# Ordering VectorE's work in a seven-product feed-forward layer by clocks of when its operands should be there

## The chip, the cores and the metric

The kernel runs on one core of one Trainium2 chip. The metric is the device time of one execution in microseconds (us); three executions of the kernel before took 946.0, 948.33 and 948.74 us, so the median is 948.33 us. One further execution was profiled, and the durations below are from it.

## The reference, cut to what matters

The model is a trunk of two layers over 256 tokens of width 1024, in float32. Each layer is a feed-forward network, a mixer (mLSTM in the first layer, windowed attention in the second) and a second feed-forward network, each with a residual and a layer norm. The change is in the feed-forward networks, of which there are four:

```python
def swiglu(x, w_in, w_out):                      # x: 256 x 1024, w_in: 1024 x 5632, w_out: 2816 x 1024
    gu = x @ w_in
    g, u = gu[..., :D_FF], gu[..., D_FF:]        # D_FF = 2816
    return (jax.nn.silu(g) * u) @ w_out

x = layer_norm(ALPHA * x + 0.5 * swiglu(x, ffn_w_in[l, i], ffn_w_out[l, i]), ...)
```

## The kernel before, in words

**Every float32 product is three matmuls.** An operand is split into a high part (rounded to the matmul's type, a cast on ScalarE, ACT) and a low part (operand minus high part, a subtraction on VectorE, DVE). `mm3` (L517) adds high x high, high x low and low x high. Weights come from memory in pieces of 128 x 1024 elements (512 KB), and each must be loaded, cast by `high` (L220, tiles `w_hi`) and subtracted by `low` (L244, tiles `w_lo`) before TensorE (PE) can use it. There are ten buffers of `w_hi` and of `w_lo` (`RING`, L27), so the splits can run up to ten pieces ahead of PE.

**A feed-forward network** (`ffn`, L657) has an opening with ordinary products, then `down` (L800), which multiplies one chunk of 128 gated columns by its rows of w_out (12 matmuls a call, results in the `py` banks), and then four blocks of `seven` (L829). A block computes 512 gate columns and 512 up columns for both halves of the tokens with seven products instead of eight, in the manner of Strassen and Winograd: sums of parts of x (tiles `S`, made once) are multiplied by sums of parts of the weights (tiles `s_raw`, formed in place). A product (`product`, L815) is 12 matmuls of 512 columns from two pieces. After each product a small function (`end1` to `end7`, L838 to L863) copies, adds, subtracts or multiplies 128 x 512 tiles, called `e` and `g` in the profile. When the gated halves `u0` and `u1` are complete, `tr` (L677) transposes them on PE (four matmuls with `ident`), and `split_evac` (L536) writes their high part (`h_hi`, ACT) and low part (`h_lo`, DVE). These are the chunks that later calls of `down` multiply.

PE's order in a full block (the first three of a network) is: product 1, transposes of the block before's `u1`, product 2, `down`, products 5 and 6, `down`, products 7 and 3, `down`, transposes of `u0` (L877), product 4, `down`. The last block has two calls of `down` fewer and does the transposes of `u0` in `end4` (L858), behind product 4. After it the filler (below) is switched off, six rows of w_out are split at once, as many pieces of the next stage are split as have buffers, and `tail` (L612) does the last chunks and the layer norm, with the transposes of the last `u1` in its midst.

**The sums of weights.** In a block, six loaded pieces (`b11`, `b12`, `b22`, two each; tiles `s_raw`) are changed step by step, and each state of them that a product needs is split. `b11` is split, has `b12` added (DVE), is split, has `b22` added (DVE), is split, has a part of the weights added straight from memory by an accumulating DMA issued from GpSimd (POOL, L273), and is split a last time, for product 4. `b12` has such a DMA too. The list `after` (filled in the planner's `seven`, L375) tells which sum follows which split.

**The order of the splits.** All is unrolled, and each engine runs its instructions in the order in which the program emits them. `Paced` (L54) keeps a model clock for PE, DVE, ACT and the loads while the program is written, and for every tile the time at which it should be there (`when`, `mark`). While a feed-forward network is emitted, `fill` (L278) is called after every matmul and adds work for ACT and DVE, as long as their clocks are less than 300 ns (`AHEAD`) past PE's: the next `high` in the order of the plan, if its raw piece was there 1000 ns ago (`SOON`) by the clocks; the first waiting sum, on the same condition; the first waiting `low`, on the same condition. The sums, the accumulating DMAs among them, wait in one list and leave it in order. The operations of `end1` to `end7` and the `h_lo` are emitted at their place at once. `take` (L298) forces what PE needs next.

The plan's order (that of the splits) is not quite that of use. `turn` and `late` in the planner's `seven` put the last split of `b11` of one block (used by its product 4) behind the first split of `b11` of the next block (used by that block's product 1), and the program keeps a list of the order of use beside it.

Of the kernel before, what the change touches and what calls it, by code (L numbers as in the profile page):

```python
# [21 lines left out]
F = 2816  # L22
# [23 lines left out]
SOON = -1000.0  # L46
LANDING = 2200.0
LOADING = 1340.0
SECOND = 1250.0
ADDING = 8000.0  # L50
# [98 lines left out]
class Weights:  # L149
# [5 lines left out]
    def __init__(self, nc, pool, words, plan, after, turns):  # L155
        self.nc, self.pool, self.words, self.plan, self.after = nc, pool, words, plan, after
        self.raw, self.parts, self.half, self.sums = {}, {}, [], []
        self.made = self.used = self.gone = 0
        self.room = 0
        self.order, self.left = turns, set(range(len(plan)))  # L160
        self.todo = {tag: [i for i, w in enumerate(words) if w["tag"] == tag] for tag in TAGS}
        self.free = {"v_raw": 0, **{tag: 0 for tag in TAGS}, "w_raw": RAW_BUFS}
        self.spool, self.send, self.vbufs = None, 0, 0
        self.uses = [0] * len(words)
# [49 lines left out]
    def split(self, upto):  # L214
        while self.made < min(upto, len(self.plan)):
            self.high()
        while self.half and self.half[0][0] < upto:
            self.low()

    def high(self):  # L220

        nc, i = self.nc, self.made
# [18 lines left out]
        self.made += 1  # L241
        return True

    def low(self):  # L244
# [15 lines left out]
        self.sums += [(i, *sum_) for sum_ in self.after.get(i, ())]  # L260
# [3 lines left out]
    def sum(self):  # L264
        nc = self.nc
        _, w, v = self.sums.pop(0)
        t = self.raw[w]
        if isinstance(v, int):
            nc.vector.tensor_add(t, t, self.raw[v])
            self.drop(v)  # L270
            self.load()
        else:
            nc.gpsimd.dma_start(t.rearrange("p (k f) -> p k f", k=self.words[w]["k"]), v, accum_op=OP.add)  # L273
            now = max(nc.vec, nc.pe)
            nc.dma = max(nc.dma, now + LANDING) + SHARE
            nc.mark(t, now + ADDING)

    def fill(self):  # L278

        nc = self.nc  # L280
        while True:
            act, vec = max(nc.act, nc.pe), max(nc.vec, nc.pe)
            if act < nc.pe + AHEAD and len(self.half) < 2 and self.made < min(self.room, len(self.plan)):
                p = self.plan[self.made]
                if (p["word"] in self.raw and nc.when(self.raw[p["word"]]) < act + SOON
                        and not any(p["needs"] == x for x in [h[0] for h in self.half] + [s_[0] for s_ in self.sums])):
                    self.high()
                    continue
            if vec < nc.pe + AHEAD:
                if self.sums and nc.when(*(self.raw[w] for w in self.sums[0][1:] if isinstance(w, int))) < vec + SOON:  # L290
                    self.sum()
                    continue
                if self.half and nc.when(self.half[0][1]) < vec + SOON:
                    self.low()
                    continue
            break

    def take(self, n):  # L298
        these = self.order[self.used:self.used + n]
        self.used += n  # L300
        self.split(max(these) + 1)
        return [self.parts[j] for j in these]
# [4 lines left out]
    def done(self, upto=None, most=None, high_only=False):  # L307
# [3 lines left out]
        while self.gone < upto:  # L311
            j = self.order[self.gone]
            self.left.discard(j)
            self.parts.pop(j, None)
            self.gone += 1
        self.room = max(self.room, min(self.left, default=len(self.plan)) + RING)
# [3 lines left out]
        end = min(self.room if most is None else min(self.room, self.made + most), len(self.plan))  # L320
        while self.made < end and self.high():
            pass
# [9 lines left out]
def trunk_kernel(ctx: ExitStack, tc: tile.TileContext, x, ffn_w_in, ffn_w_out, ln_g, ln_b, ml_w_in, ml_gate_b,  # L332
# [17 lines left out]
    def split_of(w, scale=None, needs=None):  # L350

        plan.append(dict(word=w, k=words[w]["k"], scale=scale, needs=needs, turn=len(plan)))
# [22 lines left out]
    def seven(w, c0, c1, n, down, late):  # L375
# [6 lines left out]
        first = len(plan)  # L382
        used = iter(range(99))

        def turn(n_):
            for p in plan[-n_:]:
# [1087 lines left out]
```

## Time and profile before

| what | value |
|---|---|
| time, median of three runs | 948.33 us |
| the profiled execution: its time | 948.53 us |
| the profiled execution: its span in the trace | 946.8 us |
| what lies around the span | 1.73 us |

The page of the profile shows one execution. Its first part gives each engine's busy time, share of the span and number of instructions (PEld is the load of the stationary operand, which runs beside PE's matmuls). PEclk is the clock that was granted to TensorE as a share of full speed. The view of waits says for each engine what ended its idle time: the total in us, how many times, and the longest. The timeline lists instructions in order of time: start, duration, engine, line, operation, operands, and in brackets the idle time before it and what ended it. Nearly all lines are L140, the helper that records every operation, so instructions are told apart by their tiles. The view of windows gives the busy time of each engine in a stretch, the number of instructions in brackets, and at its end the granted clock, the busy share of the DMA engines and GB/s.

### The profile page before, as it was taken

How to read it: one execution, taken by the hardware profiler on the slowest of the kernel's cores; microseconds unless marked ns; L12 is line 12 of the kernel's file. 1: busy time of each engine (PE TensorE's matmuls, PEld its weight loads, DVE VectorE, ACT ScalarE, POOL GpSimd, SP SyncE). 2: the span in 40 equal slices, each digit the busy share in tenths (PEclk: the TensorE clock that was granted, in tenths of full speed). 3: DMA queues.
4: the chain of work that ended last, by engine and by line, in shares of the span. 5: the costliest groups of instructions: out<-in, count | busy, mean ns of one | idle time of the engine just before them, and what ended most of it. 6: DMA issues, size and time to landing. Idle time of an engine off the chain costs nothing.

```text
span 946.8 us, 12553 instructions
## 1 busy us (share of the span) xinstructions
PE 918.3 (97%) x4459; PEld 763.5 (81%) x4459; DVE 810.6 (86%) x969; ACT 569.5 (60%) x793; POOL 155.5 (16%) x194
## 2 busy tenths in 40 slices
PE   9998999999999999999989999997999999999997
PEld 7786887889988888788878878886888888788885
DVE  5798998897699789999787999987868887989986
ACT  5575674645764566775535766764459564676670
POOL 0011122022321011211011111210345301212110
PEclk9998999999999999999989999999999999999999
DMA  8988997754625979987649799867343379889951
GB/s 283 354 202 272 275 283 165 239 173 151 225 95 178 335 186 321 252 251 204 218 146 356 178 278 310 252 156 235 121 156 120 104 246 287 233 224 274 290 135 45
DMA packets 100703, 208.53 MB, mean 220 GB/s; under 512 B 6904, under 2 KB 21264, under 8 KB 100640
## 3 DMA queue, kind: packets, MB, share of 16 engines
q1 hardware_dynamic: 82368, 173.04, 52.0%
q0 software_dynamic: 17696, 33.65, 20.6%
q10 hardware_dynamic: 576, 1.05, 0.3%
q8 instruction: 35, 0.57, 0.3%
q14 instruction: 28, 0.23, 0.1%
HBM read 206.65 MB, written 1.05 MB: 219 GB/s over the span
## 4 chain that ended last, share of the span: by engine, by line
PE 60%; DVE 18%; DMA 13%; issue 5%; ACT 3%; POOL 0%; SPq 0%; DVEq 0%; ACTq 0%; POOLq 0%
PE pw L140 39%; PE py L140 21%; DVE w_lo L140 11%; DMA s_raw<-in_ffn_w_in_dram 7%; DMA w_raw<-in_ffn_w_in_dram 3%; DVE e L140 2%; ACT w_hi L140 2%; DMA w_raw<-in_ffn_w_out_dram 1%; DVE s_raw L140 1%; DMA w_raw<-in_at_w_in_dram 1%; DVE h L140 1%; DVE h_lo L140 1%; POOL hrs L1111 0%; DVE x L140 0%; DVE S_lo L140 0%
## 5 line engine op out<-in xcount | busy, mean ns | idle before, releaser
L140 DVE TENSOR_TENSOR w_lo<-w_raw,w_hi 128x1024 fp32r<-128x1024 f32 (+1 forms) x213 | 254.1, 1219 | 29.6 <-ACT w_hi L140 27.6
L140 ACT CAST w_hi<-w_raw 128x1024 fp32r<-128x1024 f32 (+1 forms) x213 | 217.7, 1048 | 86.3 <-DMA w_raw<-in_ffn_w_in_dram 26.3
L140 DVE TENSOR_TENSOR w_lo<-s_raw,w_hi 128x1024 fp32r<-128x1024 f32 x192 | 228.8, 1219 | 11.5 <-ACT w_hi L140 11.4
L140 ACT CAST w_hi<-s_raw 128x1024 fp32r<-128x1024 f32 x192 | 193.4, 1052 | 59.8 <-DVE s_raw L140 55.0
L140 PE MATMUL pw<-w_hi,xT_hi 128*128 128x512 f32 x480 | 192.4, 402 | 0.0
L140 PE MATMUL pw<-w_lo,xT_hi 128*128 128x512 f32 x480 | 188.9, 395 | 3.5 <-DVE w_lo L140 3.5
L140 PE MATMUL pw<-w_hi,xT_lo 128*128 128x512 f32 x480 | 188.9, 395 | 0.0
L273 POOL DMA_DIRECT2D s_raw<-in_ffn_w_in_dram x64 | 77.4, 1209 | 503.6 <-DVE w_lo L140 190.8
L140 PE MATMUL py<-w_hi,h_hi 128*128 128x512 f32 x349 | 139.2, 399 | 3.8 <-ACT h_hi L140 3.8
L140 PE MATMUL py<-w_hi,h_lo 128*128 128x512 f32 x349 | 138.6, 397 | 3.9 <-DVE h_lo L140 3.9
L140 PE MATMUL py<-w_lo,h_hi 128*128 128x512 f32 x349 | 137.8, 395 | 0.2 <-DVE w_lo L140 0.2
L140 PEld LDWEIGHTS pw<-w_lo,xT_hi 128*128 128x128 f32 x480 | 91.5, 191 | 22.8 <-DVE w_lo L140 5.1
L140 PEld LDWEIGHTS pw<-w_hi,xT_lo 128*128 128x128 f32 x480 | 91.3, 190 | 19.9 <-DVE xT_lo L140 0.2
L140 PEld LDWEIGHTS pw<-w_hi,xT_hi 128*128 128x128 f32 x480 | 91.4, 191 | 17.6 <-issue 0.2
L140 PE MATMUL pw<-w_lo,S_hi 128*128 128x512 f32 x256 | 99.7, 389 | 0.0
L140 PE MATMUL pw<-w_hi,S_lo 128*128 128x512 f32 x256 | 99.6, 389 | 0.0
L140 PE MATMUL pw<-w_hi,S_hi 128*128 128x512 f32 x256 | 99.6, 389 | 0.0
L140 DVE TENSOR_TENSOR s_raw<-s_raw,s_raw 128x1024 f32<-128x1024 f32 x64 | 78.4, 1225 | 9.5 <-DMA s_raw<-in_ffn_w_in_dram 7.7
L140 PEld LDWEIGHTS py<-w_hi,h_lo 128*128 128x128 f32 x349 | 66.7, 191 | 19.4 <-DVE h_lo L140 5.2
L140 PEld LDWEIGHTS py<-w_hi,h_hi 128*128 128x128 f32 x349 | 66.9, 192 | 18.6 <-ACT h_hi L140 4.7
L140 PEld LDWEIGHTS py<-w_lo,h_hi 128*128 128x128 f32 x349 | 66.8, 191 | 14.4 <-DVE w_lo L140 0.6
L140 ACT CAST h_hi<-pw 128x512 fp32r<-128x512 f32 x44 | 25.7, 587 | 60.0 <-PE pw L140 60.0
(205 smaller groups left out, 1156.3 us busy)
## 6 DMA issues: line engine op xcount, KB each, us to landing
s_raw<-in_ffn_w_in_dram SPq DMA_DIRECT2D x96, 512.0 KB, 8.1
w_raw<-in_ffn_w_out_dram SPq DMA_DIRECT2D x88, 512.0 KB, 6.5
w_raw<-in_ffn_w_in_dram SPq DMA_DIRECT2D x64, 512.0 KB, 5.5
s_raw<-in_ffn_w_in_dram POOLq DMA_DIRECT2D x64, 512.0 KB, 7.6
w_raw<-in_ml_w_in_dram SPq DMA_DIRECT2D x24, 512.0 KB, 4.7
w_raw<-in_ffn_w_in_dram SPq DMA_DIRECT2D x32, 256.0 KB, 3.5
w_raw<-in_at_w_in_dram SPq DMA_DIRECT2D x12, 512.0 KB, 4.8
w_raw<-in_ml_w_out_dram SPq DMA_DIRECT2D x8, 512.0 KB, 4.3
```

The lines of the kernel that those rows point to most:

```text
L140: r = f(out, *args, **kw)
L273: nc.gpsimd.dma_start(t.rearrange("p (k f) -> p k f", k=self.words[w]["k"]), v, accum_op=OP.add)
```

## The change

1. **The plan is in the order of use.** `turn`, `late` and the second list are gone, so the last split of `b11` stands ahead of the next block's first. In place of "the next one in the plan", `fill` asks a new function `next` for a split: the first one of up to six not yet made (`LOOK`) whose raw piece should be there and which needs no split or sum that is still waiting. `high` takes the split's number.
2. **Sums.** An accumulating DMA is emitted right behind the split or the sum that it follows and no longer waits in the list; the clock takes its data as there 7000 ns later, not 8000 (`ADDING`). A piece that DVE has just added to counts as there from 700 ns ahead of DVE's clock (`NEAR`).
3. **Lows and sums on DVE.** A `low` may go when its high part was there 300 ns ago, not 1000. A sum whose split was the very last `low` lets a waiting `low` go first.
4. **A list `later`.** Low parts of transposed tiles and of the sums of x, and the DVE operations of `end2`, `end3`, `end4` and `end7`, are put on a list with the tiles that they need (`when_ready`). `fill` emits the first of the list when DVE's clock has passed the time at which those should be there; `flush` emits the whole list at once, at the start of each `down`, in `end6`, `end3`, `end4`, ahead of the transposes of `u1`, and at the end of the blocks.
5. **The transposes of `u0`** are issued in `end4` in all blocks. In the full blocks this puts them behind product 4, one product later than before; the list is flushed ahead of them, and `u1`'s product follows.

```diff
+NEAR = -700.0
+LOOK = 6
-ADDING = 8000.0
+ADDING = 7000.0
...
+    def next(self, act):
+        nc = self.nc
+        free = RING - (len(self.made) - self.gone)
+        i = self.first_left()
+        for n in range(min(LOOK, free)):
+            while i in self.made:
+                i += 1
+            if i >= len(self.plan):
+                break
+            p = self.plan[i]
+            if (p["word"] in self.raw and nc.when(self.raw[p["word"]]) < act + SOON
+                    and (p["needs"] is None or p["needs"] in self.made)
+                    and not any(p["needs"] == x for x in [h[0] for h in self.half] + [s_[0] for s_ in self.sums])):
+                return i
+            i += 1
+        return None
...
     def low(self):
...
-        self.sums += [(i, *sum_) for sum_ in self.after.get(i, ())]
+        self.fresh = i
+        sums = [(i, *sum_) for sum_ in self.after.get(i, ())]
+        while sums and not isinstance(sums[0][2], int):
+            self.transfer(*sums.pop(0)[1:])
+        self.sums += sums
...
     def sum(self):
...
+        nc.vector.tensor_add(t, t, self.raw[v])
+        nc.mark(t, nc.vec + NEAR)
...
+        while self.sums and self.sums[0][0] == i and not isinstance(self.sums[0][2], int):
+            self.transfer(*self.sums.pop(0)[1:])
...
+    def when_ready(self, f, *ins):
+        if self.nc.filler is None:
+            f()
         else:
+            self.later.append((f, ins))
+
+    def flush(self):
+        while self.later:
+            self.later.pop(0)[0]()
 
     def fill(self):
         nc = self.nc
         while True:
             act, vec = max(nc.act, nc.pe), max(nc.vec, nc.pe)
-            if act < nc.pe + AHEAD and len(self.half) < 2 and self.made < min(self.room, len(self.plan)):
-                p = self.plan[self.made]
-                if (p["word"] in self.raw and nc.when(self.raw[p["word"]]) < act + SOON
-                        and not any(p["needs"] == x for x in [h[0] for h in self.half] + [s_[0] for s_ in self.sums])):
-                    self.high()
+            if act < nc.pe + AHEAD and len(self.half) < 2:
+                i = self.next(act)
+                if i is not None:
+                    self.high(i)
                     continue
+            if self.later and nc.when(*self.later[0][1]) < vec:
+                self.later.pop(0)[0]()
+                continue
             if vec < nc.pe + AHEAD:
-                if self.sums and nc.when(*(self.raw[w] for w in self.sums[0][1:] if isinstance(w, int))) < vec + SOON:
+                add = self.sums and nc.when(*(self.raw[w] for w in self.sums[0][1:])) < vec + SOON
+                if add and self.sums[0][0] != self.fresh:
                     self.sum()
                     continue
-                if self.half and nc.when(self.half[0][1]) < vec + SOON:
+                if self.half and nc.when(self.half[0][1]) < vec - 300.0:
                     self.low()
                     continue
+                if add:
+                    self.sum()
+                    continue
             break
...
             def down(n_):
...
+                W.flush()
...
                 def end2():
-                    nc.vector.tensor_add(v["g0"], v["g0"], qc)
+                    W.when_ready(lambda: nc.vector.tensor_add(v["g0"], v["g0"], qc), qc)
...
                 def end3():
-                    nc.vector.tensor_sub(v["u0"], qb, v["u0"])
-                    nc.vector.tensor_mul(v["u0"], v["g0"], v["u0"])
+                    W.flush()
+                    W.when_ready(lambda: nc.vector.tensor_sub(v["u0"], qb, v["u0"]), qb)
+                    W.when_ready(lambda: nc.vector.tensor_mul(v["u0"], v["g0"], v["u0"]))
...
                 def end4():
                     v["g1"] = temp("g1")
                     nc.scalar.activation(v["g1"], qa, AF.Silu)
-                    if not full:
-                        tr(hB, 0, v["u0"])
-                    nc.vector.tensor_mul(v["u1"], v["g1"], v["u1"])
+                    W.flush()
+                    tr(hB, 0, v["u0"])
+                    W.when_ready(lambda: nc.vector.tensor_mul(v["u1"], v["g1"], v["u1"]), v["g1"])
...
                 product(qb, sum_("S4"), False, end3)
                 if full:
                     down(1)
-                    tr(hB, 0, v["u0"])
                 product(qa, of(4, 1), False, end4)
```

More of the change, by code (lines that the diff above doesn't have):

```diff
@@ L298, in take @@
     def take(self, n):
[L299 removed]
+        i = self.used
         self.used += n
[L301 to L302 removed]
+        self.split(self.used)
+        return [self.parts[j] for j in range(i, i + n)]
     def take_rows(self, n):
@@ L310, in done @@
         upto = self.used if upto is None else upto
[L311 to L316, printed above, removed]
+        for j in [j for j in self.parts if j < upto]:
+            del self.parts[j]
+        self.gone = max(self.gone, upto)
         if self.nc.filler is not None:
```

141 lines of the change are left out of this document (69 added, 72 removed).

## The prediction

> **What bounds the kernel now.** I read the page first: the span and the busy time of the engines.
>
> ```profile
> span 946.8 us, 12553 instructions
> PE 918.3 (97%) x4459; PEld 763.5 (81%) x4459; DVE 810.6 (86%) x969; ACT 569.5 (60%) x793; POOL 155.5 (16%) x194
> ```
>
> PE is busy for 97% of the span, so no reordering on other engines can win more than PE's idle time, 946.8 - 918.3 = 28.5 us, and what PE loses while it runs slowly. The next view is that of PE's waits.
>
> ```profile
> PE pw L140 <- DVE e L140: 7.7, 8, 2.3
> PE py L140 <- DVE h_lo L140: 3.9, 2, 2.0
> PE py L140 <- ACT h_hi L140: 3.8, 2, 3.1
> PE pw L140 <- DVE w_lo L140: 3.5, 2, 3.2
> ```
>
> Four rows hold 18.9 of the 28.5 us. The first is the transposes of `u0` (`pw<-ident,e`) waiting for the gate product `e`. The fourth is, but for 0.3 us, one wait for a low part. Where they stand is in PE's timeline, of which these are two places:
>
> ```profile
> 73.42 0.39 PE L140 MATMUL py<-w_hi,h_lo 128*128 128x512 f32 x1
> 74.73 0.63 PE L140 MATMUL pw<-ident,e 128*128 128x128 f32 x4 [0.93 <-DVE e L140]
> 75.11 0.47 PE L140 MATMUL pw<-w_hi,xT_hi 128*128 128x512 f32 x1
> 78.77 0.80 PE L140 MATMUL pw<-w_lo,xT_hi 128*128 128x512 f32 x1 [3.18 <-DVE w_lo L140]
> ...
> 83.54 0.39 PE L140 MATMUL py<-w_hi,h_hi 128*128 128x512 f32 x1
> ```
>
> ```profile
> 141.91 0.39 PE L140 MATMUL py<-w_hi,h_lo 128*128 128x512 f32 x1
> 144.20 0.63 PE L140 MATMUL pw<-ident,e 128*128 128x128 f32 x4 [1.90 <-DVE e L140]
> 144.58 0.54 PE L140 MATMUL pw<-w_hi,xT_hi 128*128 128x512 f32 x1
> ...
> 148.30 0.39 PE L140 MATMUL pw<-w_hi,xT_hi 128*128 128x512 f32 x1
> ```
>
> The reader is to see two things. A `py` matmul stands ahead of the transposes and a `pw<-..xT` matmul behind: these are the transposes of `u0` between `down` and product 4, in full blocks. And a longer wait has a tail. Nine matmuls lie between 144.58 and 148.30, 0.41 us apart, and twelve between 78.77 and 83.54. What a matmul takes undisturbed, and how long a block is at its best, the chain of waits shows:
>
> ```profile
> 343.00 5.91 PE pw L140 x28
> 348.90 2.72 PE py L140 x12
> ...
> 374.18 5.91 PE pw L140 x28
> ```
>
> Twelve matmuls of a `down` take 2.72 us, 0.227 each. A whole block, from the transposes of one `u1` to those of the next, takes 374.18 - 343.00 = 31.2 us there. So the slow stretches cost 3.72 - 9 x 0.227 = 1.7 us and 4.77 - 12 x 0.227 = 2.0 us beyond the waits. The view of windows has a third:
>
> ```profile
> 75.00:84.00 9.00, 5.82 (x19) 4.42 (x18) 7.09 (x7) 4.63 (x6) 1.20 (x1) 0.62 1.09 290
> 824.00:832.00 8.00, 5.69 (x20) 4.39 (x19) 7.31 (x8) 2.48 (x3) 0.80 (x1) 0.79 1.09 270
> 553.00:584.00 31.00, 30.99 (x141) 25.40 (x140) 29.73 (x30) 21.46 (x25) 4.82 (x4) 1.00 0.94 271
> ```
>
> The granted clock (third figure from the end) is 0.62 around the first wait and 1.00 in an undisturbed block. In the second row PE is idle for 8.00 - 5.69 = 2.31 us, the longest of the waits for `e`, and the clock of 0.79 costs 0.21 x 8 = 1.7 us more. The last row also says how much room there is: in a block of 31 us DVE is busy for 29.73 and ACT for 21.46, and the DMA engines have a share of 0.94. DVE keeps up, with 1.3 us to spare.
>
> Here the Trainium skill has a rule (TensorE: Matmul & The Clock Gate, Part 1: The HAM clock gate): the clock falls to half after an idle window of about 3.4 us and comes back after about as long at work. The length of the slow stretches agrees (3.7 us), but the trace has them behind waits of 1.90 and 2.31 us too, and the measurement decides. By the Trainium skill's idle time alone two of the three slow stretches would not be due to the waits and would stay, and the sum below would be 3.4 us higher.
>
> **The change, part by part.**
>
> *The transposes of `u0`, one product later* (part 5). Nothing is added or removed; four matmuls change places with twelve. Product 4 takes 12 x 0.227 = 2.72 us, so the gate product gets 2.72 us more. All eight waits are shorter (longest 2.31). Even if DVE changed nothing, the transposes at 144.20 would come no sooner than 141.91 + 0.23 + 2.72 = 144.86, behind the operand that freed them. Worth: -7.7 us of waits, -1.7 and -1.7 us of slow clock, together **-11.1 us**. What is late next is product 4 itself, which starts earlier and needs its low parts earlier. DVE's timeline shows when those come, in that block and in the first block of the first network:
>
> ```profile
> 140.37 2.35 DVE L140 TENSOR_TENSOR w_lo<-s_raw,w_hi 128x1024 fp32r<-128x1024 f32 x2
> ```
>
> ```profile
> 70.38 1.22 DVE L140 TENSOR_TENSOR w_lo<-s_raw,w_hi 128x1024 fp32r<-128x1024 f32 x1
> 72.03 1.23 DVE L140 TENSOR_TENSOR s_raw<-s_raw,s_raw 128x1024 f32<-128x1024 f32 x1 [0.43 <-DMA s_raw<-in_ffn_w_in_dram]
> ...
> 74.50 1.22 DVE L140 TENSOR_TENSOR w_lo<-s_raw,w_hi 128x1024 fp32r<-128x1024 f32 x1
> 75.75 1.23 DVE L140 TENSOR_TENSOR s_raw<-s_raw,s_raw 128x1024 f32<-128x1024 f32 x1
> ...
> 77.50 2.35 DVE L140 TENSOR_TENSOR w_lo<-s_raw,w_hi 128x1024 fp32r<-128x1024 f32 x2
> ```
>
> At 140.37 the pair takes 2.35 us and ends at 142.72, and product 4 would need its first piece at 142.14 + 0.23 and its second 6 x 0.227 later. The first of the pair ends at 141.6. That fits, by little.
>
> *The plan in the order of use* (part 1). The lower rows are that first block. A low, a sum, a low and a sum for the next block's first split stand ahead of the pair at 77.50, and PE got its low part when the first of that pair ended. Without those four, 2 x 1.22 + 2 x 1.23 = 4.9 us, and without the 0.43 us in which DVE waited for a load, the pair starts at about 72.2, its first low is there at 73.4 (product 4, moved ahead, would need it at 73.42 + 0.23 + 0.23 = 73.9), and the wait of 3.18 us is gone, with its slow stretch of 2.0: **-5.2 us**. What is late next: the same four operations are still to be done, in a network that has just started. DVE's lead there grew in the very time that PE stood still, and with 1.3 us to spare in 31 it cannot be won back within two blocks. Below, nothing of that comes back as a wait; above, all 5.2 us do. I give back **+3 us**, nearer to the upper end, since DVE is at its limit there.
>
> *The sums* (part 2). Emitting an accumulating DMA earlier does not issue it earlier unless it was behind another in POOL's queue, because POOL starts it when DVE's operation ends:
>
> ```profile
> 60.38 2.47 POOL L273 DMA_DIRECT2D s_raw<-in_ffn_w_in_dram  x2 [9.04 <-DVE w_lo L140]
> s_raw<-in_ffn_w_in_dram POOLq DMA_DIRECT2D x64, 512.0 KB, 7.6
> ```
>
> POOL had stood idle for 9 us before it, and SP's loads follow the lows in the same way. What changes is the clock: a split may be emitted 7000 + 1000 = 8000 ns behind the DMA, where it was 9000, and the DMAs land after 7.6 us (median). The margin falls from 1.4 to 0.4 us. ACT then sometimes stands before a piece that has not landed, with its `h_hi` copies and casts queued behind it, and DVE's lows behind those. At worst 64 x 1 us, or 4 us a block, against 1.3 us that DVE has free: 12 x 2.7 = 32 us. At best 0, for ACT is idle 9.5 of 31 us. I take 0; that row has 0.4 us left. By the Trainium skill (DMA: Bandwidth & Descriptors, Anatomy of one DMA, SWDGE path: 2.0 us and bytes over 436e3) such a DMA would be an estimated 3.2 us and the new clock harmless in any case; the row of 7.6 us speaks against that.
>
> *Lows, and the list* (parts 3 and 4). They remove waits of DVE in its own queue:
>
> ```profile
> DVE h_lo L140 <- ACT h_hi L140: 7.6, 13, 2.4
> DVE e L140 <- PE pw L140: 7.4, 11, 0.8
> DVE e L140 <- ACT g L140: 4.7, 3, 2.2
> ```
>
> The three are 19.7 us in the whole run. At best all of it goes, at worst the flush at the head of `down` puts `h_lo` and the product with `g` in front of everything, and DVE waits for two ACT operations, 0.58 us each by the `h_hi` row below, in 12 full blocks, 14 us. Either way it is DVE's time, hidden behind PE as long as its lead holds. I take 0.
>
> *The ends of the networks* are not meant to change, but 7.7 of the 18.9 us lie there:
>
> ```profile
> 472.31 1.05 ACT L140 CAST w_hi<-w_raw 128x1024 fp32r<-128x1024 f32 x1 [3.30 <-DMA w_raw<-in_ffn_w_in_dram]
> 473.26 0.58 ACT L140 CAST h_hi<-pw 128x512 fp32r<-128x512 f32 x1
> 476.58 0.79 PE L140 MATMUL py<-w_hi,h_lo 128*128 128x512 f32 x1 [1.96 <-DVE h_lo L140]
> ```
>
> ACT waits for a load of the next stage with the `h_hi` copy behind it, and PE waits for that. This occurs at two of the four ends (two waits in each of the middle rows of PE's waits): 7.7 us, and with a slow stretch like the ones above (2.0 each) about 11.7. The code there is the same, and it depends on when the last loads were issued. From -11.7 (both go) to +6 (a third end gets one); I take 0.
>
> **The sum**: -11.1 - 5.2 + 3.0 = -13.3 us against the profiled execution's 948.53 (946.8 of span and 1.73 around it), which is 0.2 us from the median. Forecast: **935.2 us**.
>
> **The rivals.**
>
> *The ends gain too.* Pieces of the next stage that are ready may now be split ahead of ones that wait for an accumulation, so their loads start earlier. For: both waits end with a load. Against: most of the stretch is emitted with the filler off. One end of two: 935.2 - 5.9 = 929.3 us.
>
> *DVE loses its lead.* If ACT stands before late accumulations for as much as DVE gains from the list, the blocks run at DVE's pace. The window of the undisturbed block speaks for it (1.3 us spare), the 19.7 us of waits that go speak against. At 1 us of extra PE wait in 8 of 16 blocks: 943.2 us.
>
> *Slower: product 4 waits for its own accumulation.* The old order had the last split of `b11` behind others and so gave its DMA time; in the order of use ACT and DVE may come to it too early or, with six ahead, fill the buffers with later pieces. In the first network the two DMAs were issued from 60.38 on and product 4 began at 75.11, 14.7 us. Landing, cast and low take 7.6 + 1.05 + 1.22 = 9.9 us for the first, and the second is 1.2 us behind: 3.6 us of margin. If that is used up, PE waits once a network as it did at 78.77, 5.2 us each, four times, of which one is there already: -11.1 + 3 x 5.2 = +4.5 us, 953.0 us; with two blocks a network it would be -11.1 + 7 x 5.2 = +25.3. It decides from the third new wait on.
>
> *The change doesn't do what it says.* If the clocks order DVE no better, the move of the transposes stays: 948.5 - 11.1 = 937.4 us. That is inside the forecast.
>
> **How the numbers follow.** Forecast with the last case, 931 to 940: 0.50. Ends gain as well, 925 to 931: 0.14. DVE loses its lead, 940 to 948: 0.16. Slower: 0.20. The range leaves out the lowest of the second case and most of the slower one: 926 to 950. The far ends of 14 and 32 us need every flush and every accumulation to be late at once, and stand in the slower case. A measurement of this kernel can tell about 0.3%, 2.8 us, from no change. Faster by more than that: 0.50 + 0.14 + 0.09 = 0.73; within it: 0.07; slower: 0.20.
>
> **What would show it.** Right: the row of PE waiting for `e` is gone or under 1 us, the wait at 78.77 has no counterpart over 1 us, and windows of the blocks show a granted clock of 1.00 and periods of 31.0 to 31.2 us in all networks. Part 4 shows in DVE's waits for ACT `g` and PE `pw`. Wrong: new rows of PE waiting for `w_lo` or `w_hi` in product 4, ACT waiting for `s_raw` DMAs in many blocks, or waits at the ends over 8 us in total.

## The result and the profile after

| what | before | after |
|---|---|---|
| time, median of 8 runs each | 947.23 us | 936.9 us |
| lowest and highest | 944.73, 949.79 us | 932.19, 942.07 us |
| the profiled execution: its time | 948.53 us | 942.07 us |
| the profiled execution: its span | 946.8 us | 940.3 us |

The ratio is 0.9892, with a 95% interval from 0.9858 to 0.9926: the kernel is faster by 1.1%. The profiled execution is the slowest of the eight, 6.5 us of span better than before, where the median is 10.3 us better. The page of the kernel after:

```profile
span 940.3 us, 12583 instructions
PE 915.2 (97%) x4459; PEld 758.6 (81%) x4459; DVE 804.3 (86%) x969; ACT 569.1 (61%) x793; POOL 155.2 (17%) x194
```

PE's idle time is 940.3 - 915.2 = 25.1 us, where it was 28.5. PE's waits (us in total, times, longest) say that nearly all of it has changed its place:

```profile
PE py L142 <- ACT h_hi L142: 5.4, 2, 4.8
PE py L142 <- DVE h_lo L142: 2.9, 5, 1.2
...
PE pw L142 <- DVE w_lo L142: 2.0, 3, 1.0
...
PE pw L142 <- DVE e L142: 1.0, 2, 0.7
```

The wait for `e`, 7.7 us in eight places, is down to 1.0 in two. The 3.5 us of waits for `w_lo` in products have become 2.0, none longer than 1.0. In their place stands one wait of 4.8 us for an `h_hi` copy. PE's timeline shows what is left around product 4 in the first network:

```profile
76.22 0.39 PE L142 MATMUL py<-w_hi,h_lo 128*128 128x512 f32 x1
77.34 0.50 PE L142 MATMUL pw<-w_hi,xT_hi 128*128 128x512 f32 x1 [0.73 <-DVE e L142]
...
140.07 0.39 PE L142 MATMUL pw<-w_hi,xT_hi 128*128 128x512 f32 x1
141.50 0.50 PE L142 MATMUL pw<-w_lo,xT_hi 128*128 128x512 f32 x1 [1.05 <-DVE w_lo L142]
```

At 77.34, where PE stood 3.18 us before, it is product 4's first matmul that waits for an operation on `e`, although it does not read `e`. DVE ran `e<-e,pw` from 76.60 to 77.28, and this reads a `pw` bank; that it is the bank into which the matmul then writes is inferred. The longest wait of a product for a low part is that at 141.50.

Since the engines' totals mix stages, I cut PE's timeline into three kinds of stretches. An *opening* runs from the end of one network to the first matmul of the next network's first block (so the mixers are in it), the *blocks* from there to the last matmul of the last product 4, an *end* from there through the 72 `py` matmuls behind it (63 in the last network). In the third network the view of windows gives these three rows before the change:

```profile
486.60:526.80 40.20, 40.20 (x186) 33.34 (x185) 31.63 (x38) 21.10 (x28) 3.88 (x3) 1.00 0.83 271
526.80:645.80 119.00, 117.94 (x532) 96.92 (x531) 111.78 (x110) 81.64 (x95) 16.84 (x14) 1.00 0.83 233
645.80:671.80 26.00, 21.04 (x90) 16.59 (x89) 18.11 (x23) 8.12 (x11) 1.46 (x1) 0.87 0.61 205
```

And after:

```profile
478.90:527.30 48.40, 42.68 (x187) 33.97 (x186) 36.29 (x44) 21.54 (x28) 3.88 (x3) 0.96 0.82 260
527.30:644.60 117.30, 117.30 (x532) 97.10 (x531) 108.67 (x108) 82.40 (x97) 16.94 (x14) 1.00 0.85 233
644.60:664.30 19.70, 18.49 (x89) 15.04 (x88) 16.09 (x21) 6.59 (x10) 1.46 (x1) 1.00 0.69 216
```

The first two figures of a row are its length and PE's busy time. The opening has grown by 8.2 us, the blocks have lost 1.7 and are without any idle time of PE, and the end has lost 6.3. The same cut through all four networks, for the profiled executions of all kernels that are told of below, gives the next table (us, summed over the networks). In it each end is counted some 0.6 us further than in the windows, to the end of the matmul behind the last `py` one, in every kernel alike, so that differences between rows are not touched. Each row is one profile; the two of the changed kernel differ by 4.1 us in the openings, 1.0 at the ends and 0.1 in the blocks.

| kernel | openings | blocks | ends | sum |
|---|---|---|---|---|
| before | 363.0 | 488.5 | 86.3 | 937.8 |
| after | 378.7 | 476.9 | 75.7 | 931.3 |
| after, profiled again (f4) | 374.6 | 476.8 | 76.7 | 928.2 |
| e1, before with part 5 alone | 363.6 | 477.1 | 96.0 | 936.7 |
| e2, after without part 5 | 374.7 | 485.0 | 72.4 | 932.2 |
| e3, after with `LOOK = 1` | 370.6 | 502.0 | 75.9 | 948.4 |
| e4, after without the list | 366.2 | 485.4 | 74.3 | 925.9 |
| f1, after, list in the blocks only | 364.1 | 475.0 | 74.2 | 913.3 |
| f2, f1 with `LOOK = 1` in openings | 365.8 | 479.8 | 73.8 | 919.4 |
| f3, after, `LOOK = 1` in last blocks | 370.6 | 486.3 | 84.0 | 941.0 |
| g1, e1 with other ends | 366.0 | 478.2 | 82.3 | 926.6 |
| g2, f1 with `ADDING = 8000` | 365.3 | 476.1 | 72.3 | 913.7 |
| g3, f1 without part 5 | 363.7 | 483.4 | 73.0 | 920.1 |
| g4, f1 with the old margins | 366.8 | 471.1 | 73.9 | 911.8 |

So the change wins 11.6 us in the blocks and 10.6 at the ends, and loses 15.7 in the openings (11.6 in f4).

### The profile page after: what moved, and what is told of

It is laid out like the page before. It is cut to its first block, busy times and chain, and to the rows that moved or that the text cites. A ratio compares the mean times of both kernels' runs of the same rounds, so it can differ in the third digit from the quotient of the medians.

```text
span 940.3 us, 12583 instructions
## 1 busy us (share of the span) xinstructions
PE 915.2 (97%) x4459; PEld 758.6 (81%) x4459; DVE 804.3 (86%) x969; ACT 569.1 (61%) x793; POOL 155.2 (17%) x194
## 3 DMA queue, kind: packets, MB, share of 16 engines
q10 hardware_dynamic: 576, 1.05, 0.3%
HBM read 206.65 MB, written 1.05 MB: 221 GB/s over the span
## 4 chain that ended last, share of the span: by engine, by line
PE 56%; DVE 17%; DMA 16%; issue 6%; ACT 4%; POOL 1%; SPq 1%; DVEq 0%; ACTq 0%; POOLq 0%
PE pw L142 35%; PE py L142 21%; DVE w_lo L142 9%; DMA s_raw<-in_ffn_w_in_dram 7%; DMA w_raw<-in_ffn_w_out_dram 4%; DMA w_raw<-in_ffn_w_in_dram 3%; ACT w_hi L142 2%; DVE s_raw L142 2%; DVE x L142 1%; DVE e L142 1%; DVE h_lo L142 1%; DVE stats L142 1%; DMA w_raw<-in_ml_w_in_dram 1%; DMA w_raw<-in_at_w_in_dram 1%; DVE h L142 1%
## 5 line engine op out<-in xcount | busy, mean ns | idle before, releaser
L142 PE MATMUL pw<-w_hi,xT_hi 128*128 128x512 f32 x480 | 189.7, 397 | 1.0 <-DVE e L142 1.0
L142 PE MATMUL pw<-w_lo,xT_hi 128*128 128x512 f32 x480 | 186.7, 390 | 1.5 <-DVE w_lo L142 1.5
L142 PE MATMUL pw<-w_hi,xT_lo 128*128 128x512 f32 x480 | 187.0, 391 | 0.8 <-DVE xT_lo L142 0.8
L142 DVE TENSOR_TENSOR s_raw<-s_raw,s_raw 128x1024 f32<-128x1024 f32 x64 | 76.4, 1219 | 1.1 <-DMA s_raw<-in_ffn_w_in_dram 1.1
L142 ACT COPY e<-pw 128x512 f32<-128x512 f32 x48 | 28.1, 586 | 58.4 <-PE pw L142 58.4
```

The lines of the kernel that those rows point to most:

```text
L142: r = f(out, *args, **kw)
```

## The experiments

All ratios are to the kernel before, on the same chip.

**e1: the move alone.** The kernel before, with nothing but part 5.

```diff
-                    if not full:
-                        tr(hB, 0, v["u0"])
+                    tr(hB, 0, v["u0"])
...
-                    tr(hB, 0, v["u0"])
```

> The kernel before with part 5 alone: the transposes of u0 stand behind product 4 in the full blocks too; plan, sums, lows and all else are old. Theory A (the prediction: it is this move that removes PE's waits for e): about 11 us faster than before, ratio 0.986 to 0.991, no wait for e over 0.5 us; the wait for w_lo in the first block of the first network stays, 3 to 5 us. Theory B (the gain comes from the new order of DVE's work, and a move on PE alone only turns the wait for e into a wait for product 4's w_lo): at most 3 us faster, ratio 0.997 or more, with 6 us or more of PE waiting for w_lo.

Measured: 947.37 us, ratio 0.9978 (0.9956 to 1.0000). The time is the one that theory B gives, but not for its reason: the waits for `w_lo` are under the 6 us that it asks for. PE's waits in e1:

```profile
PE py L140 <- DVE h_lo L140: 6.5, 5, 2.0
PE py L140 <- ACT h_hi L140: 6.1, 4, 3.0
PE pw L140 <- DVE w_lo L140: 4.9, 3, 4.4
...
PE pw L140 <- DVE e L140: 1.3, 3, 0.7
```

The wait for `e` is down from 7.7 to 1.3 us, none longer than 0.7, and the blocks are 11.4 us shorter, but the ends are 9.7 us longer: the two upper rows have grown by 4.9 us together, and slow matmuls add to it. Of the 9.7 us, 7.5 are at the end of the first network. In the windows of the kernel before it is

```profile
176.50:195.00 18.50, 18.47 (x90) 15.05 (x88) 17.16 (x22) 8.23 (x11) 1.54 (x1) 1.00 0.74 256
```

and in e1

```profile
172.80:198.80 26.00, 21.66 (x90) 15.81 (x89) 20.44 (x25) 9.19 (x12) 1.54 (x1) 0.93 0.71 233
```

PE comes to the end 3.7 us earlier (172.8 against 176.5) and leaves it 3.8 us later. What holds it is seen in ACT's timeline of e1:

```profile
185.72 1.05 ACT L140 CAST w_hi<-w_raw 128x1024 fp32r<-128x1024 f32 x1 [3.75 <-DMA w_raw<-in_ml_w_in_dram]
186.68 0.58 ACT L140 CAST h_hi<-pw 128x512 fp32r<-128x512 f32 x1
```

ACT stands before loads of the next stage, with the `h_hi` copy for PE's last rows in its queue behind the last of them. SP issued the first of these loads at 172.12, and in the kernel before at 173.39: PE comes 3.7 us earlier, the loads 1.3. (In g1, below, these copies stand ahead of the loads.)

The third row of the waits is that for the low part in the first network's product 4, in PE's timeline of e1

```profile
77.66 0.63 PE L140 MATMUL pw<-w_lo,xT_hi 128*128 128x512 f32 x1 [4.35 <-DVE w_lo L140]
```

It was 3.18 us before and has grown: product 4 comes earlier, and without part 1 its low part hardly does (77.66 against 78.77).

**e2: all but the move.** The kernel after with the transposes of `u0` at their old place.

```diff
                 def end4():
...
-                    tr(hB, 0, v["u0"])
+                    if not full:
+                        tr(hB, 0, v["u0"])
...
+                    W.flush()
+                    tr(hB, 0, v["u0"])
```

> The changed kernel without part 5: the transposes of u0 stand ahead of product 4 again in the full blocks, with a flush of the list ahead of them; all else is new. Theory A: the waits for e come back (12 places, 6 to 9 us in total, with slow stretches), the gain goes down to 0 to 4 us, ratio 0.996 to 1.000. Theory B: the clocks bring e in time, PE waits under 2 us for it and the ratio stays at 0.988 to 0.992.

Measured: 942.72 us, ratio 0.9952 (0.9925 to 0.9980). The wait for `e` is there as before:

```profile
PE pw L142 <- DVE e L142: 8.6, 5, 3.5
```

The ratio lies between the two theories; the waits are as in theory A, in five places and not twelve. Beside the kernel after the blocks have 485.0 - 476.9 = 8.1 us more, so in the blocks the move is worth that within the change. Parts 1 to 4 alone win 3.5 us in the blocks and 13.9 at the ends, and lose 11.7 in the openings: the gain of the ends and the loss of the openings are theirs.

**e3: no look ahead.** The kernel after with `LOOK = 1`: the plan in the order of use, and only its next split may go.

```diff
-LOOK = 6
+LOOK = 1
```

> The changed kernel with LOOK = 1: the next split is always the first one not made, none is taken ahead of it; all else is new. In the profile of the changed kernel PE waits for h_hi at the openings of the third and fourth network (4.8 us and 1.8 us, with slow stretches about 12 us), where casts of later pieces stand ahead of the h_hi copy on ACT. Theory C (the lookahead puts them there): the waits at the openings go, and the kernel is 5 to 12 us faster than the changed one, ratio 0.977 to 0.985. Theory D (late loads put them there, whatever the order): the openings stay as they are; and if the lookahead is what keeps the blocks supplied, PE waits for w_lo in the blocks by 5 us or more and the ratio is 0.990 to 1.000.

Measured: 961.59 us, ratio 1.0145 (1.0109 to 1.0181), slower than the kernel before and outside what either theory allowed. PE's waits:

```profile
PE pw L142 <- ACT e L142: 13.5, 11, 1.9
PE pw L142 <- DVE e L142: 8.3, 8, 2.4
```

The blocks take 502.0 us, 25.1 more than with `LOOK = 6`. In the chain of work that ended last, the `s_raw` loads hold 15% of the span, 7% before. With the other parts in place, the order of use without looking ahead is a loss. By these rows the next split in the plan is more often one whose piece is not there yet, and the copies and products of `end1` to `end7` (`e`) come too late for PE.

**e4: no list.** The kernel after, in which `when_ready` emits at once.

```diff
-        if self.nc.filler is None:
-            f()
-        else:
-            self.later.append((f, ins))
+        f()
```

> The changed kernel without the list of part 4: the low parts of transposed tiles and sums of x and the DVE operations of the ends are emitted at their place, as before. Theory A (DVE's own waits are hidden behind PE): within 3 us of the changed kernel, ratio 0.987 to 0.993, while DVE's waits for ACT g, ACT h_hi and PE pw come back (15 us or more in total). Rival (the list keeps DVE's lead): 6 us or more slower than the changed kernel, ratio 0.995 or more, with PE waiting for w_lo in the blocks.

Measured: 935.94 us, ratio 0.9872 (0.9838 to 0.9905), not to be told from the change. It looked as if the list did nothing. The table has it otherwise: without the list the blocks take 485.4 and the openings 366.2 us, with it 476.9 and 378.7. The list wins some 8.5 us in the blocks and loses about as much or more in the openings. That gave the next theory: the list should be used in the blocks alone. Its rival was that the openings suffer from looking ahead, since there splits for later rows of w_out can go ahead of what the opening needs.

**f1: the list in the blocks alone.**

```diff
-        if self.nc.filler is None:
+        if self.nc.filler is None or not self.listing:
...
+            W.listing = False          # at the start of ffn
...
+            W.listing = True           # ahead of the blocks
```

> The changed kernel with the list of part 4 in use from the blocks on and not in the openings (the stretch of a network ahead of its blocks); all else is new. In the profiles taken so far the openings of the changed kernel take 378.7 us in total against 363.0 before and 366.1 without any list, and its blocks 476.9 against 485.4 without any list. Theory G (the list delays the S and h copies in the openings, and helps in the blocks): openings 363 to 369 us, blocks 476 to 480, and 8 to 13 us faster than the changed kernel, ratio 0.975 to 0.981. Theory H (those differences are chance from profile to profile, and the list does nothing that can be measured): ratio 0.985 to 0.992, like the changed kernel and the one without a list.

Measured: 925.69 us, ratio 0.9773 (0.9746 to 0.9801); the change itself on this chip (f4) had 0.9899. So 12.1 us more are won, and this kernel beats both. PE's waits in f1, of which these are the three longest but for one of 1.7 us that all kernels have:

```profile
PE pw L142 <- DVE w_lo L142: 2.2, 2, 1.6
...
PE py L142 <- ACT h_hi L142: 1.2, 1, 1.2
PE pw L142 <- DVE e L142: 0.9, 1, 0.9
```

The openings are back at 364.1 us. In the table all five profiles of kernels that use the list in the openings (after, f4, e2, e3, f3) have 370.6 to 378.7 us there, and all nine others 363.0 to 366.8. What the list did there is seen in ACT's timeline in the opening of the fourth network, first of the kernel after:

```profile
782.69 1.05 ACT L142 CAST w_hi<-w_raw 128x1024 fp32r<-128x1024 f32 x1 [5.70 <-DMA w_raw<-in_ffn_w_in_dram]
784.92 1.05 ACT L142 CAST w_hi<-w_raw 128x1024 fp32r<-128x1024 f32 x1 [1.18 <-DMA w_raw<-in_ffn_w_out_dram]
785.88 0.61 ACT L142 CAST S_hi<-S 128x512 fp32r<-128x512 f32 x1
786.39 1.05 ACT L142 CAST w_hi<-s_raw 128x1024 fp32r<-128x1024 f32 x1
788.98 0.62 ACT L142 CAST S_hi<-S 128x512 fp32r<-128x512 f32 x1 [1.54 <-DVE S L142]
789.50 0.58 ACT L142 CAST h_hi<-pw 128x512 fp32r<-128x512 f32 x1
```

And the same place in f1:

```profile
765.96 1.05 ACT L142 CAST w_hi<-w_raw 128x1024 fp32r<-128x1024 f32 x1 [5.87 <-DMA w_raw<-in_ffn_w_in_dram]
766.91 0.61 ACT L142 CAST S_hi<-S 128x512 fp32r<-128x512 f32 x1
768.88 0.62 ACT L142 CAST S_hi<-S 128x512 fp32r<-128x512 f32 x1 [1.36 <-DVE S L142]
769.41 0.58 ACT L142 CAST h_hi<-pw 128x512 fp32r<-128x512 f32 x1
```

ACT stands before a late load in both, 5.7 and 5.9 us. Behind it f1 has the two `S_hi` and the `h_hi`, which is begun 769.41 - 765.96 = 3.45 us after the cast. After the change two casts stand between them, one of them before another late load, and it takes 789.50 - 782.69 = 6.81 us. DVE does the same with a low part:

```profile
786.52 0.69 DVE L142 TENSOR_TENSOR S_lo<-S,S_hi 128x512 fp32r<-128x512 f32 x1 [4.96 <-ACT S_hi L142]
787.13 1.22 DVE L142 TENSOR_TENSOR w_lo<-w_raw,w_hi 128x1024 fp32r<-128x1024 f32 x1
788.27 0.68 DVE L142 TENSOR_TENSOR S<-S,py 128x512 f32<-128x512 f32 x1
```

The sum of x that the second `S_hi` needs is behind that `w_lo`. PE pays for it:

```profile
790.13 0.50 PE L142 MATMUL py<-w_hi,h_hi 128*128 128x512 f32 x1 [1.67 <-DVE w_lo L142]
...
791.34 0.80 PE L142 MATMUL py<-w_hi,h_lo 128*128 128x512 f32 x1 [0.47 <-DVE h_lo L142]
...
792.53 0.63 PE L142 MATMUL py<-w_lo,h_hi 128*128 128x512 f32 x1
...
797.22 0.63 PE L142 MATMUL py<-w_hi,h_hi 128*128 128x512 f32 x1
```

That is 2.1 us of waits, and eleven steps from 792.53 to 797.22 of 0.426 us in place of 0.227, 2.2 us more. In the third network's opening, the wait of 4.8 us is of the same kind. That the list in the openings is the cause is shown by f1; by which step of the clocks it lets the casts go first was not tried.

**f2: f1, without looking ahead in the openings.**

```diff
-            W.listing = False
+            W.listing, W.look = False, 1
...
-            W.listing = True
+            W.listing, W.look = True, LOOK
```

> As the run before, with LOOK = 1 in the openings as well. Theory C (the lookahead puts casts of later pieces ahead of the S and h copies): 3 us or more faster than with the lookahead in the openings. If the list alone did it, or neither: within 3 us of the run before.

Measured: 929.20 us, ratio 0.9812 (0.9783 to 0.9842), 3.5 us slower than f1, most of it in the blocks (479.8 against 475.0). The rival falls: with the list off, looking ahead does no harm in the openings.

**f3: the kernel after, not looking ahead in the last block of each network.** This asks where the gain of the ends comes from.

```diff
+                W.look = LOOK if g < SEVENS - 1 else 1      # ahead of each block
```

> The changed kernel with LOOK = 1 in the last block of each network and LOOK = 6 elsewhere. At the ends of the second and third network (from product 4 of the last block to the last matmul of a w_out row) the kernel before takes 24.4 and 26.0 us, the one with the late transposes alone 25.4 and 26.1, the changed one 19.1 and 19.7. Theory F (in the last block the lookahead splits rows of w_out while other pieces wait for their accumulation, so buffers come free and the next stage's loads are issued 6 us earlier): those two ends are back at 23 to 27 us, and the kernel is 6 to 12 us slower than the changed one, ratio 0.996 to 1.002. Rival (the ends are short because the new order delays PE elsewhere or by other parts of the change): the ends stay under 21 us and the ratio at 0.986 to 0.992.

Measured: 953.45 us, ratio 1.0077 (1.0052 to 1.0102). This is slower than theory F allowed, and of the two ends that it named only one is back. The blocks lose 9.4 us and the ends 8.3 against the kernel after. The end of the third network is at 26.4 us again, where it was 26.0 before the change and 19.7 after; that of the second stays at 20.3 (24.4 and 19.1), behind blocks that take 4.5 us longer. SP's timeline has the first loads of the stage behind the third network. In the kernel before:

```profile
642.70 5.10 SPq L106 DMA_DIRECT2D w_raw<-in_at_w_in_dram  x3
```

After:

```profile
637.50 9.11 SPq L108 DMA_DIRECT2D w_raw<-in_at_w_in_dram  x4
```

In f3:

```profile
643.92 5.70 SPq L108 DMA_DIRECT2D w_raw<-in_at_w_in_dram  x3
```

PE reached the end of product 4 at 645.8, 644.6 and 647.2. So the loads were issued 3.1, 7.1 and 3.3 us ahead of that. The reading of this is that in the last block looking ahead splits rows of w_out that are there instead of standing before a sum, and so makes their buffers free for the next stage's loads, which have 4 us more of a lead. But the length of this end goes with that lead, and looking ahead is only one way to get it. In e3, which does not look ahead either, the end of the third network takes 19.6 us:

```profile
652.12 7.97 SPq L108 DMA_DIRECT2D w_raw<-in_at_w_in_dram  x5
```

There PE reached the end of product 4 at 657.6, 5.5 us behind the first of these loads, for its blocks were themselves late.

**f4: the kernel after again**, without an edit, on the chip of f1 to f3.

> The changed kernel itself, on the same chip as the three above, to compare them with: ratio 0.986 to 0.993; by theory G the openings of its profile take 370 us or more again, by theory H they differ from profile to profile.

Measured: 937.83 us, ratio 0.9899 (0.9873 to 0.9926). Its profile agrees with that of after in blocks and ends; of the openings, it loses 11.6 us where the other lost 15.7.

**g1: the move, and other ends.** The kernel before with part 5, and with the next stage's splits ahead of `tail` cut to two; the others are made behind the `h_hi` and `h_lo` of the last `u1`.

```diff
-            W.done(0)
+            W.done(0, 2)
...
-                        last, 4, turn)
+                        last, 4, lambda: (turn(), W.done(0)))
```

> The kernel before with part 5 alone (as in the first experiment, ratio 0.998), and at the ends of the networks only two pieces of the next stage are split ahead of the tail; the others are emitted behind the transposes of the last u1 and their h copies. Theory I (the move wins its 11 us in the blocks and gives 10 us back at the ends, because there ACT stands before loads of the next stage with the h_hi copy behind them): the waits for h_hi and h_lo at the ends go from 12 us to under 4, and the ratio falls to 0.984 to 0.991. If it is given back elsewhere (the next stage then starts short of pieces, or the ends wait for their own rows): the ratio stays at 0.995 to 1.002.

Measured: 937.61 us, ratio 0.9891 (0.9866 to 0.9916): the same as the whole change, from two small edits and none of the clocks. The ends are 82.3 us, where e1 had 96.0. The third:

```profile
641.30:663.20 21.90, 18.46 (x90) 15.09 (x89) 17.06 (x21) 8.17 (x11) 1.46 (x1) 1.00 0.60 217
```

The clock is 1.00, where it was 0.87 before. So what the move wins in the blocks is kept when nothing that PE needs at the end stands behind a load. The other ends also win something of their own, for the kernel before has 86.3 us there; the kernel before with this edit and without the move was not run.

**g2, g3, g4: f1 with one more part undone each.** g2: `ADDING` is 8000 again. g3: part 5 is undone, as in e2. g4: a `low` again goes 1000 ns after its high part, and a piece just added to is not marked as there (`NEAR`).

```diff
-ADDING = 7000.0                                     # g2
+ADDING = 8000.0
...
-                    tr(hB, 0, v["u0"])              # g3
+                    if not full:
+                        tr(hB, 0, v["u0"])
...
-        nc.mark(t, nc.vec + NEAR)                   # g4
-                if self.half and nc.when(self.half[0][1]) < vec - 300.0:
+                if self.half and nc.when(self.half[0][1]) < vec + SOON:
```

> The kernel with the list in the blocks only (ratio 0.977) with ADDING = 8000 as before. By the prediction (the clock of 7000 leaves 0.4 us of margin and costs nothing): within 3 us, ratio 0.974 to 0.981; ACT's waits for accumulating DMAs (32.0 us in the profile of the changed kernel, 4.5 before) fall to under 20 us. If the late data cost DVE its lead: 3 us or more faster. If the earlier clock is worth something: 3 us or more slower.

> The kernel with the list in the blocks only (ratio 0.977) without part 5: the transposes of u0 ahead of product 4 again. The prediction's price of the move is 11.1 us; alone on the old kernel it moved 2 us, undone on the changed kernel 5 to 6. If nothing downstream takes the gain here: 6 to 12 us slower, ratio 0.984 to 0.990, with 6 us or more of PE waiting for e. If the order of DVE's work makes it unneeded: within 3 us.

> The kernel with the list in the blocks only (ratio 0.977) with the old margins of part 3 and NEAR: a low waits until its high part was there 1000 ns ago, and a sum's result counts from its own end. By the prediction (DVE's time, hidden behind PE while the lead holds): within 3 us, ratio 0.974 to 0.981. If the splits' chain through sums is what sets the lead: 4 us or more slower, with PE waiting for w_lo.

Measured: g2 924.80 us, ratio 0.9755 (0.9733 to 0.9777); g3 930.87 us, 0.9820 (0.9799 to 0.9841); g4 923.85 us, 0.9745 (0.9718 to 0.9772). f1 had 925.69 us and 0.9773 (0.9746 to 0.9801) on another chip, so g2 and g4 are not to be told from it: the margins, and the mark on pieces just added, are worth nothing that these runs can show, and g4 has the lowest median of all, but not by more than the intervals. Without the move about 5 us are lost, and PE waits for `e` again, in g3:

```profile
PE pw L142 <- DVE e L142: 9.8, 5, 3.3
```

## Why the prediction was right in its number, and where its steps were not

The forecast was 935.2 us and the median is 936.9. But the sum of -13.3 us was for the blocks alone, with the ends and openings at nothing. The blocks gave -11.6. Two terms that were not in the sum, -10.6 at the ends and +11.6 to +15.7 in the openings, nearly cancel, so that the number came so close was luck. The kernel f1, which takes the second away, is at 925.7, so by its mechanisms the change was underestimated and its harm missed.

**The transposes of `u0`, -11.1 us: right in the blocks, wrong as a term of the whole.** e1's blocks give -11.4. But e1 gains only about 2 us, and the rival "the move stays alone" at 937.4 us was wrong by 10. The step that failed is "the ends of the networks ... I take 0", with the words "the code there is the same". An end is paced by loads; PE that arrives earlier waits there, and loses more to slow matmuls. In the change the move is worth 8.1 (e2) to 8.4 us (g3) in the blocks and about 5 to 6 us in all; here too the ends are longer with it, by 3.3 us (75.7 against 72.4 in e2) and 1.2 us (74.2 in f1 against 73.0 in g3).

**The plan in the order of use, -5.2 and +3: about right for the first network, not for all four.** Its blocks are the window

```profile
49.60:172.10 122.50, 119.24 (x533) 96.69 (x532) 113.34 (x113) 84.61 (x101) 21.82 (x23) 1.00 0.89 248
```

of the kernel after; they took 128.0 us before and 124.9 with the move alone. So the parts 1 to 4 add 2.4 us there (3.8 in f4), where the two terms gave 2.2. But in the second network the blocks take 119.6 us after the change and 117.4 with the move alone, and over all four networks it is 476.9 and 477.1: beyond the move, parts 1 to 4 together gave the blocks almost nothing. (From 78.77 to 83.54 the kernel before has eleven matmuls and not twelve, so the slow stretch there was 4.77 - 11 x 0.227 = 2.3 us and not 2.0.) The wait of 3.18 us is gone, its nearest counterparts are the 0.73 and 1.05 us shown above, and PE is idle for 3.3 us (122.50 - 119.24) in shorter waits. That these are the 3 us that were given back, by DVE's lost lead, is likely but was not shown. What the step did not say is that the order of use needs the look ahead: without it (e3) the blocks lose 25.1 us and the kernel is slower than before.

**The sums, 0: right, though what was feared took place.** ACT waits for accumulations much more often. Before and after:

```profile
ACT w_hi L140 <- DMA s_raw<-in_ffn_w_in_dram: 4.5, 3, 1.7
```

```profile
ACT w_hi L142 <- DMA s_raw<-in_ffn_w_in_dram: 32.0, 21, 4.2
```

This row was named as a sign of being wrong. In f1 it is 46.4 us, with `ADDING` at 8000 (g2) 22.4 (under 20 was expected), and the time of the two is the same; e1, with the old clock and the move alone, already has 18.5. So the clock makes only part of it. The bound of +32 us assumed that such a wait goes through ACT and DVE to PE. That it does not go there up to this size fits ACT's idle time, 9.5 of 31 us, but was not tested by itself.

**Lows and the list, 0: wrong by two terms of opposite sign.** The working looked at the blocks only and called it "DVE's time, hidden behind PE". There it won about 8.5 us (e4), within the bounds given as 19.7 and -14 us. The openings, where the same `when_ready` is called for the sums of x and the low parts, were not looked at. There DVE has no lead, copies that PE waits for share the queues with casts that wait for loads, and it cost 12.1 us (f1 against f4), 10.5 of them in the openings by the profiles (374.6 and 364.1).

**The rivals.** "The ends gain too" took place at both ends that had long waits (24.4 to 19.1 and 26.0 to 19.7), where one was priced at 5.9 us. The 10.6 us of the table are near the bound of -11.7 that the working gave if both waits went. The mechanism that it named, earlier loads, is borne out at the third network's end (f3); at the second's it is open, for there f3 stays at 20.3. The reason against it, that most of the stretch is emitted with the filler off, failed, because the loads are issued in the last block, with the filler on. "Product 4 waits for its own accumulation" did not: its waits for low parts are 2.0 us in all. "DVE loses its lead" did not either: DVE itself waits longer for high parts,

```profile
DVE w_lo L142 <- ACT w_hi L142: 60.1, 45, 5.3
```

where it was 39.6 us before, and still PE's windows in the blocks of the third network are without a gap.

**The signs that were named.** The wait for `e` fell to 1.0 us, and the longest wait of a product for a low part is 1.05: both about at their bound of 1 us. The clock in the blocks of all four networks is 1.00, and DVE's waits at `e` for ACT's `g` and PE's `pw` (4.7 and 7.4 us before) are gone: right. A period of 31 us was reached in the third and fourth networks, whose blocks take 117.3 and 117.5 us, and not in the first two, which take 122.5 and 119.6. The rows for `w_lo` in products stayed small: right. None of the signs was about the openings, which is where the time went.

## What to carry to other kernels

A gain in one stage is kept only if the next stage is not paced by something else: ask at each boundary what PE will wait for when it gets there earlier, and when those loads are issued. In an in-order queue, keep what PE is waiting for ahead of whatever may stand before a load; one such edit, with the move of the transposes (g1), was worth as much as the whole change. When a rule for the order helps in one stage, look at every other stage that calls it, and cut the time by stage before judging a part as worth nothing: e4's equal time hid 8.5 us won and about as much lost.

## What the runs showed of the hardware

Short waits cost more than themselves. The third network's end before the change has 26.00 - 21.04 = 4.96 us of idle time, and a granted clock of 0.87, which makes 3.4 us more of the 26.00. In the opening shown above waits of 1.67 and 0.47 us were followed by matmuls 0.426 us apart for over 4.7 us. Not every short wait has such a tail: behind the 1.05 us at 141.50 the matmuls are at most 0.34 us apart and soon 0.23 again.

The Trainium skill (TensorE: Matmul & The Clock Gate, Part 1: The HAM clock gate) speaks of an idle window of about 3.4 us; the waits in that opening are well under it, also together, and the measurement decides.

How long the accumulating DMAs of 512 KB take to land differs with the order of the work around them: 7.6 us (median) in the kernel before, 7.8 after, and in f1, by the DMA part of its page,

```profile
s_raw<-in_ffn_w_in_dram POOLq DMA_DIRECT2D x64, 512.0 KB, 8.5
```

which is more than the 8 us (7000 and 1000 ns by the clocks) after which a split may be emitted. ACT stood before such a piece 22 times in f1, 46.4 us in all, and f1 is still not to be told from g2, where it was 18 times and 22.4 us.
